# First feed-forward product: one 512-column stream of high and low token parts in place of two 256-column streams

## The chip, the cores and the metric

The kernel runs on one core of one Trainium2 chip. The metric is the device time of one execution, in microseconds (us). Three runs of the kernel before gave 906.57, 906.92 and 907.79 us; their median, 906.92 us, is the time that everything is compared with.

A core has five engines that run side by side and meet at semaphores: TensorE (PE in the profile; its weight loads stand apart as PEld), VectorE (DVE), ScalarE (ACT), GpSimd (POOL) and SyncE (SP), which here issues the loads of the weights.

## The reference, cut to what matters

Two layers run over 256 tokens of width 1024. In each, three token mixers are merged and normed; then comes the part that is changed:

```python
ffn = jnp.square(jax.nn.relu(x @ w_ff_in[i])) @ w_ff_out[i]     # 1024 -> 4096 -> 1024
ple = jax.nn.sigmoid(x @ w_ple_gate[i]) * (p[i] @ w_ple[i])
x = layer_norm(DEEPNORM_ALPHA * x + ffn + ple, ln2_g[i], ln2_b[i])
```

All inputs are float32. The kernel multiplies in TensorE's float32r type, so it writes each operand as a high part (a rounded copy) plus a low part (what the rounding left) and adds three of the four partial products: high by high, high weight by low token, low weight by high token.

## The kernel before, in words

The program is traced in Python and ordered once, when it is built: a list scheduler gives each engine a fixed queue, and the chip works through each queue in that order, waiting at semaphores. An instruction at the head of a queue that waits holds up all behind it.

**Tokens.** After the first norm, `x1T` holds the transposed tokens as two tiles of tag `t8k`, high and low, each [128, 8 blocks, 256 tokens] (`new_T`, L218; four buffers of 8 KB per partition). The same four buffers serve the tokens at the head of a layer (`xT`), the values of the attention (`vh`, `vl`), the merged branches (`mT`), and two constants at the start (`stage`, `sel_s`).

**Weights.** `wunit` (L194) loads 512 KB into a `wr` tile (3 buffers, issued on SP's queue), lets ACT write the high part `wh` (L175) and then DVE the low part `wl` (L176); `wh` and `wl` have 5 buffers each.

**PSUM.** Eight banks of 512 float32 columns: four of tag `ps`, four of tag `pg`. All four `pg` banks are the accumulators of the second half of the feed forward (`acc`, L904).

**The feed forward** (L903 to L954) goes in 8 chunks of 512 hidden channels. `ff_in(c)` makes a chunk's hidden channels with four weight units. For each of 8 blocks of input channels and each of 4 blocks `i` of 128 hidden channels it issues three products of 256 columns into half a `ps` bank (L916, L918, L919), 96 in all, into two `ps` banks. ACT then takes the relu of each bank (L924), POOL squares it (L926), and ACT and DVE split the square into parts (L928, which shows as L175 and L176). `ff_out(c)` multiplies these parts with four further weight units: 48 products of 512 columns into `acc` (L191).

The order of the chunks is `ff_in(0)`, `ff_in(1)`, `ff_out(0)`, `ff_in(2)`, `ff_out(1)`, and so on to `ff_out(7)`: only between `ff_in(0)` and `ff_in(1)` is there no `ff_out`.

Of the kernel before, what the change touches and what calls it, by code (L numbers as in the profile page):

```python
# [10 lines left out]
F32 = mybir.dt.float32  # L11
F32R = mybir.dt.float32r
# [4 lines left out]
P = 128  # L17
# [12 lines left out]
# the order of the projections, and of what goes on between their units: (job, steps to the next)  # L30
# [13 lines left out]
# columns of the combined projection  # L44
# [7 lines left out]
def hybrid_trunk(ctx, tc, x, p, w_in, b_forget, w_up_fox, w_up_sb, w_up_dsa, w_out,  # L52
# [29 lines left out]
    def t8k(dt=F32R):  # L82
        return act.tile([P, 2048], dt, tag="t8k", name=nm("t8k"), bufs=4)
# [43 lines left out]
    stage = act.tile([P, 768], F32, tag="t8k", name="stage", bufs=4)  # L127
# [6 lines left out]
    # -1 where row > column  # L134
# [3 lines left out]
    # [1 where row <= column | 1]  # L138
# [6 lines left out]
    # +BIG where column > row, over [tile 0 | tile 1: 0, diagonal]  # L145
# [4 lines left out]
    # per head h, rows h and 32 + h: ones; rows 64 + h and 96 + h: the parts of -c of the queries  # L150
    sel = cst.tile([P, H_FOX, T], F32R, name="sel")
    sel_s = act.tile([P, H_FOX, T], F32, tag="t8k", name="sel_s", bufs=4)
# [19 lines left out]
    def split(src, hi, lo, scale=None):  # L172
        """src * scale as two float32r parts, whose sum is exact."""
        if scale is None:
            a = nc.scalar.copy(hi, src)  # L175
            b = nc.vector.tensor_sub(lo, src, hi.bitcast(F32))  # L176
            if pinned[0]:
                pinned[0] -= 1
                tc.keep_in_program_order(a)
                tc.keep_in_program_order(b)  # L180
        else:
            nc.scalar.activation(hi, src, AF.Copy if isinstance(scale, float) else AF.Identity,
                                 scale=scale)
            nc.vector.scalar_tensor_tensor(lo, src, scale, hi.bitcast(F32),
                                           op0=ALU.mult, op1=ALU.subtract)

    def mm3(o, a, b, start, stop, skip=False):
        """o += a.T @ b from the parts (hi, lo) of each."""
        prods = ((a[0], b[0]), (a[0], b[1]), (a[1], b[0]))
        for i, (l, r) in enumerate(prods):  # L190
            nc.tensor.matmul(o, l, r, start=start and i == 0, stop=stop and i == 2,  # L191
                             skip_group_check=skip)

    def wunit(srcs, nk, n):  # L194
        """Weights [P, nk, n] on chip, as parts; srcs: list of (partition slice, dram AP)."""
        raw = early.pop(0) if early else wload(srcs, nk, n)
        hi = wp.tile([P, nk, n], F32R, tag="wh", name=nm("wh"), bufs=WH)
        lo = wp.tile([P, nk, n], F32R, tag="wl", name=nm("wl"), bufs=WH)
        split(raw, hi, lo)
        return hi, lo  # L200

    def transpose_to(dst, src_list):
        """src_list: blocks [P, 128] -> the columns of psum tile dst."""
        for i, s in enumerate(src_list):
            tr = nc.tensor.transpose(dst[:, i * P:(i + 1) * P], s, ident)  # L205
            if behind:
                tc.keep_in_program_order(tr)
                behind.pop()

    def to_T(src, t, hT, lT):  # L210
        """src [P, 1024] of token tile t -> hT, lT [P, 8, 256] at its columns."""
        for g in range(2):
            q = ps()
            transpose_to(q, [src[:, (4 * g + i) * P:(4 * g + i + 1) * P] for i in range(4)])
            qv = q.rearrange("p (k t) -> p k t", t=P)
            split(qv, hT[:, 4 * g:4 * g + 4, t * P:(t + 1) * P], lT[:, 4 * g:4 * g + 4, t * P:(t + 1) * P])

    def new_T():  # L218
        return (t8k().rearrange("p (k t) -> p k t", t=T), t8k().rearrange("p (k t) -> p k t", t=T))
# [4 lines left out]
    def xstat(aT, w, l, c0, n, done, nkb=KB, nk=2, by_tile=False, mid=None):  # L224
        """done(t, psum tile) with the [tokens, n] products of token tile t; a step per unit.
        By tile: all of tile 0 first, mid() after it; the high parts of the tokens come first."""
# [45 lines left out]
    def layer_norm(t, st, gt, bt, done, out_pieces=()):  # L272
        """xs[t] <- layer norm of itself, half by half (or by pieces, to out), from its statistics."""
# [28 lines left out]
    def half_T(hT, lT):  # L302
        """What turns half j of xs[t] into its transposed parts."""
        def f(t, j):
            q = ps()
            transpose_to(q, [xs[t][:, (4 * j + i) * P:(4 * j + i + 1) * P] for i in range(4)])
            qv = q.rearrange("p (k t) -> p k t", t=P)
            split(qv, hT[:, 4 * j:4 * j + 4, t * P:(t + 1) * P], lT[:, 4 * j:4 * j + 4, t * P:(t + 1) * P])
        return f

    def ple_products(l, pn):
        """p w_ple, [tokens, 1024] by half and token tile, half by half."""
# [20 lines left out]
    # x transposed  # L333
# [6 lines left out]
    for l in range(L):  # L340
        if l:
            tc.keep_in_program_order(nc.scalar.preload_act_table_set("natural_log_exp_and_others"))
        vh = t8k()[:, 0:1792].rearrange("p (t c) -> p t c", t=2)
        vl = t8k()[:, 0:1792].rearrange("p (t c) -> p t c", t=2)

        def do_rope(t, src, nh, dst, dup=1):
            """dst [P, nh * 64] <- rope of the nh heads at src (psum)."""
# [131 lines left out]
        M = {}  # L479

        def idx_scores(t):
            nk = (t + 1) * P
            sc = act.tile([P, 256], F32, tag="sc", name=nm("sc"), bufs=2)
            n_in = 512 // nk  # heads in a bank, of one row tile
# [70 lines left out]
        # outputs of pairs of heads as parts (high, low); of the heads 10 and 11 as stacks [high; low]  # L555
# [3 lines left out]
        def values(n, m, pT):  # L559
            """The outputs of the heads n .. n + m - 1 (of all 16; one block), into oT, from the  # L560
            parts of their weights [keys, m, 384]: keys of tile 0 for all queries, keys of tile 1
            for tile 1's."""
# [16 lines left out]
        def softmax_heads(n, heads, mask):  # L579
            """heads: (parts of qT [64, 256] scaled by -SCALE, parts of kT [64, 256], extra) each."""  # L580
# [24 lines left out]
            for i in range(len(heads)):  # L605
                q = ps()
                # psum: keys of tile 0 x (queries 0, queries 1), keys of tile 1 x queries 1
# [27 lines left out]
        def sb_unit(kb):  # L635
            """Columns [sq, sk] as [sq 01, sq 23, sk 01, sk 23, sq 4 | sk 4]."""
# [18 lines left out]
        def strict(a, m):  # L655
            """a [P, m, 384] <- 0 where the key isn't before the query."""
# [5 lines left out]
        def sb_heads(hs):  # L662
# [26 lines left out]
            # sums over the later keys: those of tile 0 within it and over tile 1, those of tile 1  # L689
# [47 lines left out]
        def up_blocks(j, kbs, w, n0=0):  # L737
            """Adds the blocks kbs of heads, with the weights at columns n0 .. of w."""
# [39 lines left out]
        # the branch that comes first and its first block, the last block of each branch  # L778
# [32 lines left out]
        # job: (the products that it needs, steps before the next job, job)  # L811
# [40 lines left out]
        # a zero that comes with the last head's weights: no sigmoid between the exponentials  # L852
# [11 lines left out]
        x1T = new_T()  # L864
# [39 lines left out]
        acc = [[pg() for _ in range(2)] for _ in range(2)]  # L904

        def ff_in(c):
            pz = [ps(), ps()]
            for u in range(4):
                wt = wunit(wrows(w_ff_in, l, 2 * u, 2, c * 512, 512), 2, 512)
                for kk in range(2):  # L910
                    kb = 2 * u + kk
                    for i in range(4):
                        o = pz[i // 2][:, (i % 2) * T:(i % 2 + 1) * T]
                        hi, lo = (w[:, kk, i * P:(i + 1) * P] for w in wt)
                        rh, rl = x1T[0][:, kb, :], x1T[1][:, kb, :]
                        nc.tensor.matmul(o, hi, rh, start=kb == 0 and i % 2 == 0, stop=False,  # L916
                                         skip_group_check=True)
                        nc.tensor.matmul(o, hi, rl, start=False, stop=False, skip_group_check=True)  # L918
                        nc.tensor.matmul(o, lo, rh, start=False, stop=kb == KB - 1,  # L919
                                         skip_group_check=True)  # L920
            hs = []
            for i in range(2):
                r = t2k(F32)
                nc.scalar.activation(r, pz[i], AF.Relu)  # L924
                h = t2k(F32)
                nc.gpsimd.tensor_mul(h, r, r)  # L926
# [33 lines left out]
        for t in range(2):  # L960
            # the last tile's last half in two pieces
# [23 lines left out]
def _rope_table():  # L985
    """[128, (cos tile 0, cos tile 1, sin tile 0, sin tile 1), 64], by the positions alone."""
# [26 lines left out]
```

## Time and profile before

| | us |
|---|---|
| median of three runs | 906.92 |
| lowest, highest run | 906.57, 907.79 |
| span of the profiled execution (first to last instruction) | 907.9 |
| PE busy in the span | 890.1 (98%) |
| DVE busy | 610.4 (67%) |
| ACT busy | 475.5 (52%) |
| POOL busy | 116.1 (13%) |

Of the profiled execution only its span is recorded; it lies 0.1 us above the highest of the three runs. Of a PE row the start is what counts: products overlap in the pipeline, so a row's duration (0.28 us for 256 columns) is longer than the distance from one start to the next (0.12 us), and it is the distance that adds up to time.

### The profile page before, as it was taken

The numbers are of one execution on the slowest core, as the hardware profiler recorded it, in microseconds if no ns is written. First come the engines' busy times: TensorE is split into PE (matmuls) and PEld (weight loads), VectorE is DVE, ScalarE is ACT, GpSimd is POOL, SyncE is SP. The second block draws the span as 40 slices with busy tenths as digits, with TensorE's granted clock in tenths as the row PEclk, the third lists the DMA queues.
The fourth block names the chain that finished last, engine by engine and source line by source line (L and its number), as shares of the span: only waits on it lengthen the run. The fifth ranks groups of instructions, "written<-read, shape, count | busy, mean of one in ns | idle before, by whom it ended". The sixth has DMA issues, their size and how long they took to land.

```text
span 907.9 us, 13848 instructions
## 1 busy us (share of the span) xinstructions
PE 890.1 (98%) x5190; PEld 778.7 (86%) x5190; DVE 610.4 (67%) x1035; ACT 475.5 (52%) x719; POOL 116.1 (13%) x155
## 2 busy tenths in 40 slices
PE   6999999999999999999999999999999999999996
PEld 5999988887779999999879999788777899999995
DVE  6578888678876544444676888876789564444446
ACT  4455656766445444444355555576844454444440
POOL 5002110200012011111200120101000321111120
PEclk9999999999999999999999999999999999999999
DMA  6655465452656766656636546555346576666662
GB/s 199 197 158 128 143 188 150 137 180 93 186 178 216 210 187 186 186 187 187 218 104 200 150 120 171 158 161 166 115 143 201 167 228 190 187 187 187 186 200 75
DMA packets 79699, 154.51 MB, mean 170 GB/s; under 512 B 10096, under 2 KB 25456, under 8 KB 79632
## 3 DMA queue, kind: packets, MB, share of 16 engines
q1 hardware_dynamic: 77952, 149.04, 54.7%
q0 software_dynamic: 1680, 4.60, 1.8%
q8 instruction: 41, 0.67, 0.3%
q14 instruction: 26, 0.21, 0.1%
HBM read 152.30 MB, written 1.05 MB: 169 GB/s over the span
## 4 chain that ended last, share of the span: by engine, by line
PE 44%; DVE 3%; issue 1%; DMA 1%; ACT 1%; POOLq 0%; POOL 0%; ACTq 0%; SPq 0%; DVEq 0%
PE pg L191 23%; PE ps L919 3%; PE ps L918 3%; PE ps L916 3%; PE ps L191 3%; PE pg L233 1%; PE pg L389 1%; PE pg L391 1%; PE pg L392 1%; DVE wl L176 1%; PE pg L238 1%; DMA wr<-in_w_out_dram 1%; PE ps L205 0%; DMA wr<-in_w_in_dram 0%; PE pg L749 0%
## 5 line engine op out<-in xcount | busy, mean ns | idle before, releaser
L176 DVE TENSOR_TENSOR wl<-wr,wh 128x1024 fp32r<-128x1024 f32 (+5 forms) x303 | 350.7, 1162 | 236.0 <-ACT wh L175 234.7
L175 ACT CAST wh<-wr 128x1024 fp32r<-128x1024 f32 (+5 forms) x303 | 296.2, 982 | 309.1 <-PE pg L191 107.7
L191 PE MATMUL pg<-wh,t8k 128*128 128x512 f32 (+4 forms) x768 | 224.5, 365 | 0.0
L191 PE MATMUL pg<-wh,t2k 128*128 128x512 f32 x544 | 172.8, 394 | 1.4 <-ACT wh L175 1.2
L191 PEld LDWEIGHTS pg<-wh,t8k 128*128 128x128 f32 x768 | 140.0, 188 | 19.7 <-issue 0.5
L919 PE MATMUL ps<-t8k,wl 128*128 128x256 f32 x512 | 144.9, 283 | 0.0
L918 PE MATMUL ps<-t8k,wh 128*128 128x256 f32 x512 | 144.9, 283 | 0.0
L916 PE MATMUL ps<-t8k,wh 128*128 128x256 f32 x512 | 144.8, 283 | 0.0
L191 PE MATMUL pg<-wl,t8k 128*128 128x512 f32 (+4 forms) x384 | 138.8, 362 | 0.0
L191 PEld LDWEIGHTS pg<-wh,t2k 128*128 128x128 f32 x544 | 103.0, 190 | 23.6 <-ACT wh L175 2.1
L191 PE MATMUL pg<-wl,t2k 128*128 128x512 f32 x272 | 107.3, 395 | 2.2 <-DVE wl L176 2.2
L918 PEld LDWEIGHTS ps<-t8k,wh 128*128 128x128 f32 x512 | 98.2, 192 | 0.6
L916 PEld LDWEIGHTS ps<-t8k,wh 128*128 128x128 f32 x512 | 98.2, 192 | 0.6
L919 PEld LDWEIGHTS ps<-t8k,wl 128*128 128x128 f32 x512 | 98.2, 192 | 0.0
L191 PEld LDWEIGHTS pg<-wl,t8k 128*128 128x128 f32 x384 | 72.2, 188 | 7.9
L926 POOL TENSOR_TENSOR t2k<-t2k 128x512 f32<-128x512 f32 x32 | 40.6, 1270 | 273.9 <-ACT t2k L924 258.6
L191 PEld LDWEIGHTS pg<-wl,t2k 128*128 128x128 f32 x272 | 51.6, 190 | 13.5 <-DVE wl L176 3.4
L389 PE MATMUL pg<-t8k,wh 128*128 128x256 f32 x176 | 50.6, 287 | 0.0
L392 PE MATMUL pg<-t8k,wl 128*128 128x256 f32 x176 | 49.8, 283 | 0.0
L391 PE MATMUL pg<-t8k,wh 128*128 128x256 f32 x176 | 49.7, 283 | 0.0
L233 PE MATMUL pg<-wh,t8k 128*128 128x512 f32 x96 | 37.9, 400 | 1.0 <-ACT t8k L175 1.0
L233 PE MATMUL pg<-wl,t8k 128*128 128x512 f32 x96 | 37.9, 398 | 0.6 <-DVE small L276 0.2
(180 smaller groups left out, 1077.5 us busy)
## 6 DMA issues: line engine op xcount, KB each, us to landing
wr<-in_w_ff_in_dram SPq DMA_DIRECT2D x64, 512.0 KB, 3.8
wr<-in_w_ff_out_dram SPq DMA_DIRECT2D x64, 512.0 KB, 3.6
wr<-in_w_in_dram SPq DMA_DIRECT2D x48, 512.0 KB, 3.7
wr<-in_w_in_dram SPq DMA_DIRECT2D x32, 384.0 KB, 3.5
wr<-in_w_out_dram SPq DMA_DIRECT2D x16, 512.0 KB, 3.9
wr<-in_w_ple_gate_dram SPq DMA_DIRECT2D x16, 512.0 KB, 4.5
wr<-in_w_in_dram SPq DMA_DIRECT2D x16, 256.0 KB, 2.8
wr<-in_w_in_dram SPq DMA_DIRECT2D x8, 390.0 KB, 3.5
```

The source lines that it names most:

```text
L175: a = nc.scalar.copy(hi, src)
L176: b = nc.vector.tensor_sub(lo, src, hi.bitcast(F32))
L191: nc.tensor.matmul(o, l, r, start=start and i == 0, stop=stop and i == 2, skip_group_check=skip)
L233: nc.tensor.matmul(o[t][:, :n], tok(aT, u * nk + kk, t)[0], wt[i][:, kk, :], start=u + kk + i == 0, stop=False)
L238: nc.tensor.matmul(o[t][:, :n], tok(aT, kb, t)[1], units[kb // nk][0][:, kb % nk, :], start=False, stop=kb == nkb - 1)
L389: nc.tensor.matmul(oi, hi, rh, start=kb == 0 and i % 2 == 0, stop=False, skip_group_check=True)
L391: nc.tensor.matmul(oi, hi, rl, start=False, stop=False, skip_group_check=True)
L392: nc.tensor.matmul(oi, lo, rh, start=False, stop=kb == KB - 1, skip_group_check=True)
L916: nc.tensor.matmul(o, hi, rh, start=kb == 0 and i % 2 == 0, stop=False, skip_group_check=True)
L918: nc.tensor.matmul(o, hi, rl, start=False, stop=False, skip_group_check=True)
L919: nc.tensor.matmul(o, lo, rh, start=False, stop=kb == KB - 1, skip_group_check=True)
L926: nc.gpsimd.tensor_mul(h, r, r)
```

## The change

One pool tag is widened: `t8k` (four buffers of 8 KB) becomes `t16k` (two buffers of 16 KB), so that the high and the low part of the tokens lie in one tile, 8 KB apart, and one access pattern can run over both. Every user of the tag changes with it. In `ff_in` the two products that use the high weights become one of 512 columns, high tokens then low tokens, into a whole `ps` bank, so a chunk takes all four `ps` banks in place of two. The third product is as before and adds into the first half. Afterwards ACT copies the low half of each bank to SBUF and DVE adds the high half to it; the relu and the square are one DVE instruction in place of ACT's relu and POOL's product.

```diff
-    def t8k(dt=F32R):
-        return act.tile([P, 2048], dt, tag="t8k", name=nm("t8k"), bufs=4)
+    def t16k(dt=F32R):
+        return act.tile([P, 2, 2048], dt, tag="t16k", name=nm("t16k"), bufs=2)
...
     def new_T():
-        return (t8k().rearrange("p (k t) -> p k t", t=T), t8k().rearrange("p (k t) -> p k t", t=T))
+        return both_T()[0]
+
+    def both_T():
+        a = t16k().rearrange("p i (k t) -> p i k t", t=T)
+        return (a[:, 0], a[:, 1]), a
...
-        x1T = new_T()
+        x1T, x1_both = both_T()
...
         def ff_in(c):
-            pz = [ps(), ps()]
+            pz = [ps() for _ in range(4)]
             for u in range(4):
                 wt = wunit(wrows(w_ff_in, l, 2 * u, 2, c * 512, 512), 2, 512)
                 for kk in range(2):
                     kb = 2 * u + kk
                     for i in range(4):
-                        o = pz[i // 2][:, (i % 2) * T:(i % 2 + 1) * T]
                         hi, lo = (w[:, kk, i * P:(i + 1) * P] for w in wt)
-                        rh, rl = x1T[0][:, kb, :], x1T[1][:, kb, :]
-                        nc.tensor.matmul(o, hi, rh, start=kb == 0 and i % 2 == 0, stop=False,
-                                         skip_group_check=True)
-                        nc.tensor.matmul(o, hi, rl, start=False, stop=False, skip_group_check=True)
-                        nc.tensor.matmul(o, lo, rh, start=False, stop=kb == KB - 1,
-                                         skip_group_check=True)
+                        nc.tensor.matmul(pz[i].rearrange("p (k t) -> p k t", t=T), hi, x1_both[:, :, kb, :],
+                                         start=kb == 0, stop=False, skip_group_check=True)
+                        nc.tensor.matmul(pz[i][:, 0:T], lo, x1T[0][:, kb, :], start=False,
+                                         stop=kb == KB - 1, skip_group_check=True)
             hs = []
             for i in range(2):
                 r = t2k(F32)
-                nc.scalar.activation(r, pz[i], AF.Relu)
+                for k in range(2):
+                    z, rk = pz[2 * i + k], r[:, k * T:(k + 1) * T]
+                    nc.scalar.copy(rk, z[:, T:2 * T])
+                    nc.vector.tensor_add(rk, z[:, 0:T], rk)
                 h = t2k(F32)
-                nc.gpsimd.tensor_mul(h, r, r)
+                nc.vector.scalar_tensor_tensor(h, r, 0.0, r, op0=ALU.max, op1=ALU.mult)
                 pr = (t2k(), t2k())
                 split(h, *pr)
```

The values `vh` and `vl` of the attention and the two constants at the start (`stage`, `sel_s`) move to the new tag as well. The rest of the diff takes out comments.

## Rows read from the trace of the kernel before

**Rows 1.** The page, section 1: busy time, share of the span, instructions.

```profile
PE 890.1 (98%) x5190; PEld 778.7 (86%) x5190; DVE 610.4 (67%) x1035; ACT 475.5 (52%) x719; POOL 116.1 (13%) x155
```

**Rows 2.** Both first chunks, layer 0: length, PE to POOL busy, clock, DMA, GB/s.

```profile
275.40:298.40 23.00, 23.00 (x193) 22.99 (x192) 16.21 (x14) 12.64 (x16) 6.31 (x4) 1.00 0.70 213
```

**Rows 3.** Timeline of PE: first products of the first four half-chunks (start, duration, line).

```profile
275.41 0.28 PE L916 MATMUL ps<-t8k,wh 128*128 128x256 f32 x1
...
286.92 0.28 PE L916 MATMUL ps<-t8k,wh 128*128 128x256 f32 x1
...
298.44 0.40 PE L191 MATMUL pg<-wh,t2k 128*128 128x512 f32 x1
...
309.35 0.28 PE L916 MATMUL ps<-t8k,wh 128*128 128x256 f32 x1
```

**Rows 4.** Timeline of PE: twelve products over gapped operands, and the next.

```profile
646.26 2.25 PE L191 MATMUL ps<-t3k,t8k 128*128 128x512 f32 x12
648.35 0.40 PE L191 MATMUL pg<-wh,t1k 128*128 128x512 f32 x1
```

**Rows 5.** Timeline of ACT after ff_in(0) of layer 0, brackets: idle before, releaser.

```profile
287.26 1.05 ACT L175 CAST wh<-wr 128x1024 fp32r<-128x1024 f32 x1 [1.73 <-DMA wr<-in_w_ff_in_dram]
288.21 0.59 ACT L924 ACTIVATE t2k<-ps 128x512 f32<-128x512 f32 x1
288.70 1.04 ACT L175 CAST wh<-wr 128x1024 fp32r<-128x1024 f32 x1
...
291.03 0.59 ACT L924 ACTIVATE t2k<-ps 128x512 f32<-128x512 f32 x1
```

**Rows 6.** Timeline of DVE in the same stretch.

```profile
288.34 1.23 DVE L176 TENSOR_TENSOR wl<-wr,wh 128x1024 fp32r<-128x1024 f32 x1 [1.56 <-ACT wh L175]
```

**Rows 7.** Timeline of SP: issue of the load behind the cast at 287.26.

```profile
282.36 0.37 SPq L97 DMA_DIRECT2D wr<-in_w_ff_in_dram  x1
```

**Rows 8.** The same place in layer 1: PE, ACT, DVE.

```profile
731.99 0.28 PE L916 MATMUL ps<-t8k,wh 128*128 128x256 f32 x1
...
732.39 1.05 ACT L175 CAST wh<-wr 128x1024 fp32r<-128x1024 f32 x1 [1.78 <-DMA wr<-in_w_ff_in_dram]
733.34 0.59 ACT L924 ACTIVATE t2k<-ps 128x512 f32<-128x512 f32 x1
...
733.47 1.23 DVE L176 TENSOR_TENSOR wl<-wr,wh 128x1024 fp32r<-128x1024 f32 x1 [1.60 <-ACT wh L175]
```

**Rows 9.** Lines by form: count, busy us, mean ns, idle before, releasers.

```profile
L175 ACT CAST t2k<-pg 128x256 fp32r<-128x256 f32 x6 | 2.0, 373 | 0.1
L176 DVE TENSOR_TENSOR t2k<-pg,t2k 128x256 fp32r<-128x256 f32 x6 | 2.3, 416 | 0.0
L893 DVE SCALAR_TENSOR_TENSOR x<-x,t2k 128x512 f32<-128x512 f32 x8 | 5.5, 690 | 7.1 <-POOL t2k L891 7.1
```

**Rows 10.** The last chunk: timelines of ACT and DVE, chain of waits.

```profile
877.51 0.60 ACT L924 ACTIVATE t2k<-ps 128x512 f32<-128x512 f32 x1 [1.23 <-PE ps L919]
...
883.21 0.68 DVE L176 TENSOR_TENSOR t2k<-t2k,t2k 128x512 fp32r<-128x512 f32 x1
...
878.19 16.36 PE pg L191 x72
```

**Rows 11.** Start of the span: PE at 9 and 17 us, DVE, ACT.

```profile
9.16 0.63 PE L191 MATMUL pg<-wh,t2k 128*128 128x512 f32 x1
9.59 0.63 PE L191 MATMUL pg<-wl,t2k 128*128 128x512 f32 x1
...
17.24 0.39 PE L233 MATMUL pg<-wh,t8k 128*128 128x512 f32 x1
17.47 0.39 PE L233 MATMUL pg<-wl,t8k 128*128 128x512 f32 x1
...
4.99 1.48 DVE L162 CAST cT<-stage 64x128 fp32r<-64x128 f32 x1
...
15.44 0.59 ACT L175 CAST t8k<-ps 128x512 fp32r<-128x512 f32 x1 [0.27 <-PE ps L205]
```

More of the change, by code (lines that the diff above doesn't have):

```diff
@@ L126, in hybrid_trunk @@
     nc.vector.memset(eps_t[0:64, 1:2], SCALE)
-    stage = act.tile([P, 768], F32, tag="t8k", name="stage", bufs=4)
+    stage = act.tile([P, 768], F32, tag="t16k", name="stage", bufs=2)
     def tri(ap, n, keep, fill, op, base, cm, step):
@@ L151, in hybrid_trunk @@
     sel = cst.tile([P, H_FOX, T], F32R, name="sel")
-    sel_s = act.tile([P, H_FOX, T], F32, tag="t8k", name="sel_s", bufs=4)
+    sel_s = act.tile([P, H_FOX, T], F32, tag="t16k", name="sel_s", bufs=2)
     nc.gpsimd.memset(sel_s, 0.0)
@@ L342, in hybrid_trunk @@
             tc.keep_in_program_order(nc.scalar.preload_act_table_set("natural_log_exp_and_others"))
-        vh = t8k()[:, 0:1792].rearrange("p (t c) -> p t c", t=2)
-        vl = t8k()[:, 0:1792].rearrange("p (t c) -> p t c", t=2)
+        vhl = t16k()[:, :, 0:1792].rearrange("p i (t c) -> p i t c", t=2)
+        vh, vl = vhl[:, 0], vhl[:, 1]
         def do_rope(t, src, nh, dst, dup=1):
```

## The prediction

> **What bounds the kernel now.** I read the busy shares first: PE is busy 98% of the span, DVE 67%, ACT 52% [rows 1]. A share is only an average, so the table by stretches comes next: in the two first chunks of layer 0, PE is busy 23.00 of 23.00 us at a granted clock of 1.00, with the DMA engines at 0.70 [rows 2]. PE alone sets the time there, and work on ACT, DVE or POOL costs time only where PE comes to wait for it.
>
> Then the timeline of PE, read by starts. A first-half chunk takes 286.92 - 275.41 = 11.51 us for 96 products of 256 columns, 0.1199 us each; a second-half chunk 309.35 - 298.44 = 10.91 us for 48 products of 512 columns, 0.2273 us each [rows 3]. Twice the columns cost less than twice the time: the line through both points is 0.4195 ns per column and 12.5 ns per product. Those 12.5 ns are what this change can win.
>
> **What the change removes.** Per chunk, 64 products of 256 columns become 32 of 512: 32 x (2 x 0.1199 - 0.2273) = 0.40 us, and 0.40 x 16 chunks in both layers = 6.4 us, all of it on the bound engine. The new moving operand has two runs 8 KB apart, which the second half's operands have not. The nearest row is the weighted sum of the attention's values, whose moving operand also has two gapped runs: six products of 512 columns and six of 256 take 648.35 - 646.26 = 2.09 us, 0.348 us for a pair of one each [rows 4], where the two averages above make 0.347. So the gap is free there, and by this row the gain is 16 x (11.51 - 32 x 0.348) = 6.0 us. I take 6.4 and keep 5.9 to 6.4.
>
> The Trainium skill has a smaller price for a product: TensorE: Matmul & The Clock Gate, section "Wait — 56ns, not 53.3ns?", gives a fixed cost of about 2.5 ns on top of the columns. By it the estimate would be 512 x 2.5 ns = 1.3 us in place of 6.4. The distances above disagree by a factor of five, and they decide.
>
> **What it adds.** Each chunk now fills four `ps` banks, and there are four. Between most chunks this costs nothing: a second half of 10.91 us, which writes only `pg` banks, lies between one first half and the next, and emptying the banks is shorter. In the last chunk, where the squares are needed soonest, the work from ACT's first read at 877.51 to DVE's last part at 883.21 + 0.68 = 883.89 fits into 6.4 us [rows 10]; the change turns two reads of 512 columns into four copies at 0.373 us on ACT and four additions at 0.416 us on DVE, and moves the squares from POOL to DVE at about 0.69 us each [rows 9]. That is 4 x 0.416 + 2 x 0.69 = 3.0 us more for DVE; even in series it ends by 887, and the second half that reads these squares begins 10.9 us after 878.19, at 889.1. Cover: that second half. If it were gone, 6 to 9 us per chunk would show.
>
> It is gone once per layer: `ff_in(1)` follows `ff_in(0)` directly. Before, the second one took the two free banks; now its first product needs the bank that ACT and DVE must first empty. So a wait is added on PE, and behind it on PE's queue stands all that follows.
>
> **How long that wait is.** Shortened, `ff_in(0)` ends at 275.41 + 11.11 = 286.52. On ACT's queue of before, the relu of the first bank is not next: a weight cast for `ff_in(1)` stands ahead of it, waits 1.73 us for its transfer and runs from 287.26; the relu comes at 288.21, though its bank was complete at 286.92 - 0.84 + 0.28 = 286.36 (the last product into it is seven before the next chunk's first [rows 3]) [rows 5]. That transfer was issued at 282.36 [rows 7] and does not depend on PE's pace, so it lands no sooner after the change. On DVE the subtraction of the same weights runs 288.34 to 289.57 [rows 6]. If the scheduler keeps the order, the first copy starts at 288.2 and the first addition only at 289.5; the bank is free at 289.5 + 0.42 = 289.95, and PE has waited 3.4 us. In layer 1 the end is 731.99 - 0.40 = 731.59, the subtraction ends at 733.47 + 1.23 = 734.70, the bank is free at about 735.05: 3.5 us [rows 8]. Behind the first bank the second keeps PE's pace of 0.35 us, but the first square (0.69 us, ready then and earlier in program order) probably precedes the third bank's addition. That adds 0.65 us, or nothing if PE's queue is filled with products of the free banks instead, or up to 2.0 if the cast at 288.70 (1.04 us [rows 5]) and its subtraction also come between. I take 0.65, since squares stand before later banks in the program.
>
> Sum: 2 x (3.45 + 0.65) - 6.4 = +1.8 us, between 2 x 3.4 - 6.4 = +0.4 and 2 x 5.5 - 5.9 = +5.1. The span of 907.9 lies 1.0 above the median; I apply the difference to the median: 908.7, with 907.3 to 912.0.
>
> The Trainium skill speaks against the change here: Perfetto Trace Analysis, section "Matmuls", wants independent groups to rotate through PSUM banks, so that one is emptied while the next is written. Here it holds in 14 of 16 chunks only.
>
> **Edits with one answer.** Square on DVE: POOL's 32 products go and DVE has 33% idle. The wider tag: the pairs were taken and freed together before, so it changes nothing but the start, where `xT` now reuses the buffer of `stage`; its last reader ends at 6.47 us and `xT` is first written at 15.44 [rows 11]. If the scheduler put that reader later, it could cost up to 1 us.
>
> **Rivals.**
> - *The copies overtake the cast* (the other side: faster). The queue order is fixed when the kernel is built. If all four copies stand ahead of that weight cast, the first bank is copied and added while `ff_in(0)` still writes the last: it is complete some 0.9 us before the end, and 0.373 + 0.416 us fit. What remains per layer is the third and fourth bank, 0.5 to 1.3 us. Time: -6.4 + 1.0 to -5.9 + 2.6, so 901.5 to 903.6, about 902.5. For it: a copy precedes the cast in program order, and the first bank is ready earlier than the relu's two halves were. Against it: the cast stood ahead of the relu in both layers [rows 5, 8]. It decides by whether the cast is ready, in the order made at build time, before the first bank is.
> - *Half of that*: the first copies ahead, the rest behind the cast, or one layer each way. Wait about 2.4 us per layer: 906.9 - 6.4 + 4.8 = 905.3 (904.5 to 907).
> - *The wait lowers PE's clock.* The rows of before hold no idle time of PE near 3.5 us except at the start, where products of 512 columns start 0.43 us apart at 9 us, the lower level of 1.2 GHz (though the row's granted clock says 1.00), and 0.23 us apart at 17 us [rows 11]. If 5.2 us of streaming after each wait ran at that level, it would cost 2 x 2.6 us on top of the forecast: 913.9, and with half of that 911.3. For it: between 275 and 298 us PE has no idle time at all [rows 2], so the trace can't vouch for a wait there. The Trainium skill's page TensorE: Matmul & The Clock Gate (section "What's actually happening") says that an idle TensorE falls to half rate; no run here shows it for a wait of this length.
> - *The long product does not stream.* If two runs 8 KB apart cost as much as two products, nothing is won and 2 x 4.1 us are lost: 915.1. Against it stand rows 4. With the 2.5 ns of the Trainium skill (the page named above) it would be near 913.8, which I count here.
>
> **How the numbers follow.** Forecast 46%, copies overtake 23%, half 12%, clock 14%, no gain 5%. About 0.2% (1.8 us) is what a measurement of this kernel can tell from no change: the bounds are 905.1 and 908.7. Faster: 23 + 4 (of the half) = 27%. Same: 20 (of the forecast) + 8 = 28%. Slower: 26 + 14 + 5 = 45%. The range takes the overtaking case down to 902.0 and the clock case to 912.5; outside it lie 5% below and some 11% above. The forecast's own range is 907.3 to 912.0.
>
> **What would show it.** Step one: a first-half chunk behind a second half takes 11.1 us from start to start, and pairs of products start 0.347 us apart. Step two: PE's waits list about 3.5 us twice, on its first product of `ff_in(1)`, released by DVE's addition, and nowhere else. Step three: on ACT the copies stand behind the cast that waits for its transfer. The prediction is wrong if the copies stand ahead of it (then near 902.5), if other chunks wait for banks, if products behind the wait start 0.43 us apart, or if the long product takes over 0.23 us.

## The result and the profile after

| | before | after |
|---|---|---|
| median of all runs (us) | 907.27 (906.57 to 909.31, 10 runs) | 913.26 (907.9 to 914.68, 10 runs) |
| ratio to before, 95% interval | 1 | 1.0056 (1.0043 to 1.007) |
| span of the profiled execution | 907.9 | 911.6 (its own time 913.28) |

The change makes the kernel 6.0 us slower by the two medians, and 5.1 us by the ratio, which is not the quotient of the medians. The forecast was 908.7 with a range to 912.5: the side is right, the size is not. The median lies 0.8 us above that range; but the range was set against 906.92, and counted from there (+6.0 against +5.6 by the medians, 1.0056 x 906.92 = 912.0 by the ratio) the time lies at its upper end.

The page's line of busy times answers to [rows 1]. The second line is the page's group of the new long product (count, busy us, mean ns, idle time before it and its releaser):

```profile
PE 888.5 (97%) x4678; PEld 752.4 (83%) x4678; DVE 651.4 (71%) x1131; ACT 478.8 (53%) x751; POOL 75.6 (8%) x123
...
L921 PE MATMUL ps<-t16k,wh 128*128 128x512 f32 x512 | 184.3, 403 | 6.1 <-DVE t2k L931 6.1
```

PE has 512 instructions fewer, and 6.1 us of idle time that it had not. PE's list of waits (engine and line, what it waited for: total us, times, longest) says where; its other waits are those at the kernel's other stages, and none is in the feed forward:

```profile
PE ps L921 <- DVE t2k L931: 6.1, 2, 3.4
PE ps L322 <- DMA pn<-in_p_dram: 3.8, 1, 3.8
PE pg L192 <- DVE wl L177: 1.2, 1, 1.2
PE pg L192 <- ACT wh L176: 1.2, 1, 1.2
```

Two waits, one in each layer, both on the first product of `ff_in(1)`, both ended by an addition. In PE's timeline (start, duration, line, operands; brackets: idle before, releaser) the end of `ff_in(0)` and the products behind the wait, first layer 0, then layer 1:

```profile
283.94 0.40 PE L921 MATMUL ps<-t16k,wh 128*128 128x512 f32 x1
284.17 0.28 PE L923 MATMUL ps<-t16k,wl 128*128 128x256 f32 x1
287.07 0.50 PE L921 MATMUL ps<-t16k,wh 128*128 128x512 f32 x1 [2.62 <-DVE t2k L931]
...
288.74 0.63 PE L921 MATMUL ps<-t16k,wh 128*128 128x512 f32 x1
289.17 0.41 PE L923 MATMUL ps<-t16k,wl 128*128 128x256 f32 x1
289.38 0.63 PE L921 MATMUL ps<-t16k,wh 128*128 128x512 f32 x1
...
731.65 0.28 PE L923 MATMUL ps<-t16k,wl 128*128 128x256 f32 x1
735.37 0.67 PE L921 MATMUL ps<-t16k,wh 128*128 128x512 f32 x1 [3.44 <-DVE t2k L931]
735.84 0.41 PE L923 MATMUL ps<-t16k,wl 128*128 128x256 f32 x1
736.05 0.63 PE L921 MATMUL ps<-t16k,wh 128*128 128x512 f32 x1
...
736.69 0.63 PE L921 MATMUL ps<-t16k,wh 128*128 128x512 f32 x1
```

From start to start, less the usual 0.12 us behind a short product, PE loses 287.07 - 284.17 - 0.12 = 2.78 us and 735.37 - 731.65 - 0.12 = 3.60 us. Then comes a second loss: at 288.74 and at 736.05 a pair of products takes 0.64 us instead of 0.353. The table by stretches shows the clock (length; busy us of PE, PEld, DVE, ACT, POOL with counts; granted clock; DMA share; GB/s). The four stretches are `ff_in(0)` and `ff_in(1)` of layer 0, then of layer 1:

```profile
273.00:284.30 11.30, 11.30 (x65) 9.69 (x63) 8.06 (x7) 4.97 (x6) 3.25 (x2) 1.00 0.70 219
287.00:300.00 13.00, 12.93 (x65) 11.15 (x65) 8.89 (x14) 5.67 (x9) 0.00 (x0) 0.87 0.45 143
720.40:731.80 11.40, 11.40 (x66) 9.73 (x64) 8.40 (x8) 5.56 (x7) 3.66 (x2) 1.00 0.65 199
735.30:748.30 13.00, 12.93 (x65) 11.20 (x66) 8.90 (x14) 5.67 (x9) 0.00 (x0) 0.87 0.46 143
```

Before, the clock was 1.00 and PE busy throughout here [rows 2]. Now the same 64 products take 12.93 us behind the wait and 11.29 without one, with the clock at 0.87 on average: part of the stretch ran at 1.2 GHz. That is 2 x 1.64 = 3.3 us.

The gain shows in the twelve first halves that stand alone. The first product of one, and that of the second half behind it (compare [rows 3], where 11.51 us lie between them):

```profile
310.89 0.39 PE L921 MATMUL ps<-t16k,wh 128*128 128x512 f32 x1
311.12 0.28 PE L923 MATMUL ps<-t16k,wl 128*128 128x256 f32 x1
311.23 0.40 PE L921 MATMUL ps<-t16k,wh 128*128 128x512 f32 x1
...
322.18 0.40 PE L192 MATMUL pg<-wh,t2k 128*128 128x512 f32 x1
...
333.12 0.39 PE L921 MATMUL ps<-t16k,wh 128*128 128x512 f32 x1
```

322.18 - 310.89 = 11.29 us, the same in all twelve: 0.22 us per chunk, 3.5 us for sixteen, where 0.40 and 6.4 were forecast. The second half behind it takes 333.12 - 322.18 = 10.94 us instead of 10.91; over both layers the second halves give back 0.3 us.

The sum, without those 0.3 us: -3.5 + (2.78 + 3.60) + 3.3 = +6.2 us, against +6.0 between the medians. The spans differ by 3.6 only, because this profiled execution of after was 2.4 us ahead before the feed forward: its `ff_in(0)` starts at 273.00, that of before at 275.41 [rows 3], as PE came to its upper clock earlier at the start of the span. That differs from run to run (b3 below, a changed kernel, starts its `ff_in(0)` at 275.51) and is no part of the change. In the runs where both are recorded a time is 1.6 to 1.8 us above its span, so the profiled execution of before, with a span of 907.9, took about 909.6 us, which fits its late start.

### The profile page after: what moved, and what is told of

Read it like the earlier page. It is cut to its first block, busy times and chain, and to the rows that moved or that the text cites. A ratio compares the mean times of both kernels' runs of the same rounds, so it can differ in the third digit from the quotient of the medians.

```text
span 911.6 us, 12926 instructions
## 1 busy us (share of the span) xinstructions
PE 888.5 (97%) x4678; PEld 752.4 (83%) x4678; DVE 651.4 (71%) x1131; ACT 478.8 (53%) x751; POOL 75.6 (8%) x123
## 4 chain that ended last, share of the span: by engine, by line
PE 43%; DVE 3%; DMA 2%; issue 1%; ACT 1%; POOL 1%; POOLq 0%; ACTq 0%
PE pg L192 22%; PE ps L921 6%; PE ps L192 3%; PE ps L923 3%; PE pg L239 1%; DVE wl L177 1%; PE pg L395 1%; PE pg L398 1%; PE pg L397 1%; DMA wr<-in_w_ff_in_dram 1%; PE pg L244 1%; ACT wh L176 1%; PE ps L206 1%; POOL t2k L897 0%; DMA wr<-in_w_out_dram 0%
## 5 line engine op out<-in xcount | busy, mean ns | idle before, releaser
L192 PE MATMUL pg<-wh,t16k 128*128 128x512 f32 (+4 forms) x768 | 224.4, 365 | 0.0
L921 PE MATMUL ps<-t16k,wh 128*128 128x512 f32 x512 | 184.3, 403 | 6.1 <-DVE t2k L931 6.1
L192 PEld LDWEIGHTS pg<-wh,t16k 128*128 128x128 f32 x768 | 140.0, 188 | 19.7 <-issue 0.5
L923 PE MATMUL ps<-t16k,wl 128*128 128x256 f32 x512 | 144.8, 283 | 0.0
L192 PE MATMUL pg<-wl,t16k 128*128 128x512 f32 (+4 forms) x384 | 138.8, 362 | 0.0
L921 PEld LDWEIGHTS ps<-t16k,wh 128*128 128x128 f32 x512 | 97.5, 191 | 30.7 <-DVE t2k L931 6.7
L923 PEld LDWEIGHTS ps<-t16k,wl 128*128 128x128 f32 x512 | 98.2, 192 | 0.7
L192 PEld LDWEIGHTS pg<-wl,t16k 128*128 128x128 f32 x384 | 72.2, 188 | 7.9
L395 PE MATMUL pg<-t16k,wh 128*128 128x256 f32 x176 | 50.6, 288 | 0.0
L397 PE MATMUL pg<-t16k,wh 128*128 128x256 f32 x176 | 49.7, 283 | 0.0
L395 PEld LDWEIGHTS pg<-t16k,wh 128*128 128x128 f32 x176 | 33.6, 191 | 0.3
L397 PEld LDWEIGHTS pg<-t16k,wh 128*128 128x128 f32 x176 | 33.7, 191 | 0.0
```

Of the source, the lines that this page charges most:

```text
L395: nc.tensor.matmul(oi, hi, rh, start=kb == 0 and i % 2 == 0, stop=False, skip_group_check=True)
L397: nc.tensor.matmul(oi, hi, rl, start=False, stop=False, skip_group_check=True)
L921: nc.tensor.matmul(pz[i].rearrange("p (k t) -> p k t", t=T), hi, x1_both[:, :, kb, :], start=kb == 0, stop=False, skip_group_check=True)
L923: nc.tensor.matmul(pz[i][:, 0:T], lo, x1T[0][:, kb, :], start=False, stop=kb == KB - 1, skip_group_check=True)
```

## The experiments

All times are medians beside the kernel before on the same chip (907.13, 907.45, 906.99 and 906.94 us for the groups a, b, c and d); the bracket is the 95% interval of the ratio to it, which again is not the quotient of the two medians.

| label | median | ratio to before | first half (us) |
|---|---|---|---|
| a1_change_again | 914.03 | 1.0063 (1.0046 to 1.0081) | 11.29 |
| a2_first_two_as_before | 905.21 | 0.9976 (0.9966 to 0.9986) | 11.29 |
| a3_fill_the_wait | 909.67 | 1.0029 (1.0019 to 1.0039) | 11.29 |
| a4_one_run | 913.89 | 1.0063 (1.0047 to 1.008) | 11.29 |
| b1_split_on_pool | 911.41 | 1.0041 (1.0027 to 1.0055) | 11.29 |
| b2_swap_banks | 903.65 | 0.9958 (0.9946 to 0.9971) | 11.29 |
| b3_swap_low_products_grouped | 904.42 | 0.9958 (0.9946 to 0.997) | 11.20 |
| b4_swap_low_products_one_late | 903.53 | 0.9955 (0.9942 to 0.9968) | 11.29 |
| c1_swap_grouped_one_run | 902.31 | 0.995 (0.9937 to 0.9963) | 11.20 |
| c2_swap_banks_again | 904.13 | 0.9964 (0.9951 to 0.9976) | 11.29 |
| d1_swap_groups_of_8 | 901.33 | 0.9942 (0.9927 to 0.9956) | 11.15 |
| d2_swap_groups_of_16 | 900.61 | 0.9943 (0.9924 to 0.9962) | 11.11 |

### The change again

> The changed kernel once more, timed beside the three experiments on the same chip. Expected 5 to 6.5 us above the kernel before: a gain of 0.22 us in each of 16 first-half chunks (3.5), against two waits of 2.8 and 3.6 us and twice 1.65 us in which the chunk behind the wait runs at a lower clock. If the difference to the kernel before is under 3 us, the first comparison was a matter of the chip or of the hour.

6.9 us above before. In its profiled execution the waits cost 3.17 and 3.43 us and `ff_in(1)` 13.93 and 12.79 us: -3.5 + 6.6 + 4.1 = +7.2. The two waits add up to much the same (6.4 and 6.6); what follows them at the lower clock does not (1.5 to 2.6 us per layer in the two profiles), which fits the wide spread of after's times.

### Where the loss sits

```diff
-            pz = [ps() for _ in range(4)]
+            short = c < 2
+            pz = [ps() for _ in range(2 if short else 4)]
...
+                        if short:
+                            o = pz[i // 2][:, (i % 2) * T:(i % 2 + 1) * T]
...
+                            nc.tensor.matmul(o, hi, rl, start=False, stop=False, skip_group_check=True)
...
+                if short:
+                    nc.scalar.activation(r, pz[i], AF.Relu)
```

> The first two chunks of each layer keep the three products of 256 columns in two banks and the relu on ScalarE; the other six are as changed. So no first half needs a bank that is still being emptied. Theory (waits and the clock behind them cost 9.7 us, each long-product chunk gains 0.22): no wait on an addition in PE's list, the granted clock stays 1.00 between 270 and 300 us, and the time is that of before less 12 x 0.22 = 2.7 us. Rival (the long product itself, or VectorE's larger load, makes the kernel slower): above the kernel before, by about 12/16 of the change's loss.

1.9 us below before, interval 1.3 to 3.1, which holds the 2.7 of the theory. The wait on the addition is gone from PE's list, and the second chunk, like the first, is again what it was:

```profile
284.70:296.20 11.50, 11.50 (x98) 11.50 (x97) 8.35 (x9) 7.76 (x10) 0.00 (x0) 1.00 0.70 218
```

So the long product, the copies, the additions and the squares on DVE gain in twelve chunks; all of the loss comes from the two chunks in each layer that follow each other directly.

### The clock, apart from the wait

```diff
+            if c == 1:
+                for _ in range(12):
+                    nc.tensor.matmul(acc[0][0].rearrange("p (k t) -> p k t", t=T), last_w[0],
+                                     x1_both[:, :, 0, :], start=True, stop=True, skip_group_check=True)
```

In `ff_in(1)` the loop also takes the first two banks through three weight blocks before the other two, since the queue of the changed kernel, too, works on the first two banks for a while before it touches the third.

> The changed kernel, with twelve additional products of 512 columns (2.8 us at 0.235 each) between ff_in(0) and ff_in(1), written to an accumulator that the first real product of ff_out(0) overwrites. They use operands that are there already, so PE streams during the wait in place of idling, while ACT and VectorE empty the banks in the same queue order. Theory (idling lowers the clock, and that costs 1.65 us per layer by itself): the products behind the wait start at the pace of 0.353 us per pair, the granted clock stays at 1.00, and the time is 3.3 us below that of the changed kernel. Rival (the lower clock there has another cause, such as the change of operands or of banks): the clock falls as before and the time is not below that of the changed kernel.

4.4 us below the changed kernel. The products that fill the wait, and what comes behind them:

```profile
284.20 2.94 PE L919 MATMUL pg<-t16k,wl 128*128 128x512 f32 x12
287.25 0.50 PE L934 MATMUL ps<-t16k,wh 128*128 128x512 f32 x1
287.58 0.28 PE L936 MATMUL ps<-t16k,wl 128*128 128x256 f32 x1
287.70 0.40 PE L934 MATMUL ps<-t16k,wh 128*128 128x512 f32 x1
287.94 0.28 PE L936 MATMUL ps<-t16k,wl 128*128 128x256 f32 x1
288.06 0.40 PE L934 MATMUL ps<-t16k,wh 128*128 128x512 f32 x1
```

The table by stretches, for `ff_in(1)`:

```profile
287.20:298.70 11.50, 11.45 (x65) 9.95 (x66) 8.90 (x13) 5.66 (x9) 0.00 (x0) 1.00 0.43 143
```

PE is held up about as long as in after (287.25 - 284.20 = 3.05 us, and 2.78 in layer 1), but it streams meanwhile; behind it pairs start about 0.355 us apart and the clock is 1.00. Idling, not the new operands or banks, lowers the clock here. From `ff_in(0)` to the end of `ff_in(1)` the two layers take 25.75 and 25.45 us, 6.0 more than four chunks of 11.29; -3.5 + 6.0 = +2.5, and the median is +2.5 above before. The 4.4 us to a1 are about what the lower clock cost there (4.1 by the traces) and its longer waits (6.6 against 6.0). The Trainium skill, TensorE: Matmul & The Clock Gate, section "What's actually happening", has an idle TensorE fall to half rate; this pair of runs agrees.

### The queue order in front of the copies

```diff
+                if c == 1 and u == 3:
+                    raw = wload(wrows(w_ff_in, l, 2 * u, 2, c * 512, 512), 2, 512)
...
+                    nc.gpsimd.tensor_copy(wt[0], raw)
+                    nc.gpsimd.tensor_sub(wt[1], raw, wt[0].bitcast(F32))
```

> The changed kernel, with the split of the last weight block of ff_in(1) (cast and subtraction) on GpSimd in place of ScalarE and VectorE, in both layers. The four copies and additions that empty the banks then have no weight cast ahead of them that waits for its transfer. Theory (the wait is long because the copies stand behind that cast): the wait on the addition falls from 2.6 and 3.4 us to under 1 us per layer, the clock does not fall, and the time is about 905 us (907.1 - 16 x 0.22 + 2 x 0.8 = 905.2). Rival (the wait is the work of emptying itself, wherever the cast stands): the wait stays above 2 us, and the time stays near that of the changed kernel, 913 to 914. A third outcome: GpSimd needs so long for the split that the products of that block wait for it, near the end of ff_in(1).

Neither theory nor rival: 911.41. The first wait falls as the theory says, and a second one takes its place. Timelines of layer 0 (L928 is the long product, L938 the addition, L921 here GpSimd's subtraction):

```profile
284.20 0.75 DVE L938 TENSOR_TENSOR t2k<-ps,t2k 128x256 f32<-128x256 f32 x2
...
284.67 0.50 PE L928 MATMUL ps<-t16k,wh 128*128 128x512 f32 x1 [0.23 <-DVE t2k L938]
...
286.59 1.05 ACT L176 CAST wh<-wr 128x1024 fp32r<-128x1024 f32 x1 [2.44 <-DMA wr<-in_w_ff_out_dram]
...
286.66 2.39 POOL L921 TENSOR_TENSOR wl<-wr,wh 128x1024 fp32r<-128x1024 f32 x1
...
287.67 2.46 DVE L177 TENSOR_TENSOR wl<-wr,wh 128x1024 fp32r<-128x1024 f32 x1 [1.99 <-ACT wh L176]
...
290.65 0.74 DVE L938 TENSOR_TENSOR t2k<-ps,t2k 128x256 f32<-128x256 f32 x2
...
291.21 0.47 PE L928 MATMUL ps<-t16k,wh 128*128 128x512 f32 x1 [2.86 <-DVE t2k L938]
```

The two subtractions in layer 1, and then the stretches behind the second wait in layer 0 and in layer 1:

```profile
731.99 2.73 POOL L921 TENSOR_TENSOR wl<-wr,wh 128x1024 fp32r<-128x1024 f32 x1
733.14 2.67 DVE L177 TENSOR_TENSOR wl<-wr,wh 128x1024 fp32r<-128x1024 f32 x1 [0.68 <-ACT wh L176]
...
291.20:299.00 7.80, 7.79 (x45) 6.86 (x46) 5.56 (x8) 4.49 (x6) 0.00 (x0) 1.00 0.59 190
737.00:746.00 9.00, 9.00 (x44) 7.82 (x45) 5.34 (x7) 4.47 (x6) 0.00 (x0) 0.84 0.52 162
```

With no cast ahead of them the copies and additions of the first two banks are done at once, and PE waits 0.23 us. But the next cast in ACT's queue, for the second half's weights, also waits for its transfer; its subtraction stands on DVE ahead of the additions for the third and fourth bank, and takes 2.46 us instead of 1.23. PE runs out of products for the first two banks and waits 2.86 us (2.47 in layer 1). The two chunks take 26.04 and 27.08 us, 8.0 more than four of 11.29: -3.5 + 8.0 = +4.5, measured +4.0. So the split ahead of the copies and additions (the cast on ACT with its subtraction on DVE) set the length of the first wait: shown. Getting ahead of it did not win the wait back here.

The subtraction is slow only in the shadow of GpSimd's: it ends 290.13, 1.08 us after GpSimd's at 286.66 + 2.39 = 289.05; in layer 1 likewise, 735.81 after 734.72. The Trainium skill, SBUF — State Buffer, section "SBUF: two separate sides", says that a VectorE instruction with two SBUF inputs and a GpSimd one that reads SBUF lock each other out for a whole instruction. Both places agree; there the split could not be moved free of charge. So part of the second wait is this run's own doing. An estimate takes off what the subtraction took too long, 2.46 - 1.23 = 1.23 us in layer 0 and 1.44 in layer 1; 1.6 and 1.0 us of the second waits are left, which the next cast in the queue would have caused by itself.

### Another bank instead of a shorter wait

```diff
+    role = ["ps", "pg"]
...
-        return psp.tile([P, 512], F32, tag="ps", name=nm("ps"), bufs=4)
+        return psp.tile([P, 512], F32, tag=role[0], name=nm("ps"), bufs=4)
...
+            if c == 1:
+                role.reverse()
             hs = ff_in(c)
+            if c == 1:
+                acc += [[pg() for _ in range(2)] for _ in range(2)]
```

`pg()` takes its tag from `role[1]` in the same way, and the accumulators are taken only behind `ff_in(1)`, so that `ff_in(1)` writes the four banks that `ff_in(0)` has not touched.

> All 16 first halves as changed, but before ff_in(1) of each layer the two sets of four banks change roles: ff_in(1) takes the four that are still free, and the accumulators of the second half take those that ff_in(0) has used, once they are emptied. Theory (only the bank makes ff_in(1) wait): no wait on an addition, the granted clock stays 1.00, ff_in(1) takes 11.3 us, and the time is 907.1 - 16 x 0.22 = 903.6 us. Rival (with the two first halves back to back, ff_in(1) waits for its weights instead, at ScalarE and VectorE, which have no pause there): the time stays above 905.2.

903.65, as the theory says; once more with c2: 904.13.

> The changed kernel with swapped banks once more, to compare with the grouped one on the same chip. Expected: 903 to 904.5 us, 11.29 us per first half.

The stretch of `ff_in(1)` in layer 0 of b2, with no wait in front of it and none in it:

```profile
284.50:295.80 11.30, 11.30 (x66) 9.80 (x65) 8.94 (x13) 7.71 (x13) 0.00 (x0) 1.00 0.58 196
```

The weights are there in time: ACT 7.71 and DVE 8.94 of 11.30 us busy. Layer 1 is the same, 11.30 us at a clock of 1.00. So the wait was for the bank alone.

### The missing half of the gain

The forecast took 0.347 us for a pair of one long and one short product; it is 0.353. Where do the 6 ns come from? First, one run of 512 columns in place of two:

```diff
-        a = t16k().rearrange("p i (k t) -> p i k t", t=T)
-        return (a[:, 0], a[:, 1]), a
+        a = t16k().rearrange("p i n -> p (i n)").rearrange("p (k i t) -> p k i t", i=2, t=T)
+        return (a[:, :, 0], a[:, :, 1]), a
```

> The changed kernel, with the transposed tokens laid out so that the high and the low part of one block stand side by side: the 512 columns of the long product are one run instead of two runs 8 KB apart. The waits stay. Theory (the second run costs about 6 ns per product): a first-half chunk behind a second half takes 11.1 us instead of 11.29, and the time is 16 x 0.18 = 2.9 us below that of the changed kernel. Rival (the pair costs 0.353 us for another reason, such as the alternation of lengths): the chunk stays at 11.29 and the time does not move.

11.29 us still, and no difference to a1. The gap of 8 KB costs nothing here. Next, in b4 each short product comes one product later, so that no two products into one bank follow each other, and in b3 the four long products of a block come first and the four short ones behind them:

> The kernel with the swapped banks; each product of 256 columns comes one product later than before, so lengths still alternate but two products into the same bank never follow each other. If the bank is what costs the 6 ns per pair, a first half takes 11.1 us; if the turn of lengths does, 11.29, while the grouped order gains; if both stay at 11.29, it is neither.

> The kernel with the swapped banks; in each block of tokens the four products of 512 columns come first and the four of 256 columns after them, in place of one of each in turn. So seven of eight products follow one of their own length, and none follows a product into the same bank. The pair has cost 0.353 us where a row of equal products makes 0.347. Theory A (the surplus of 6 ns comes from the turn of lengths or from two products into one bank behind each other): a first half takes 11.15 us instead of 11.29, and the time is 16 x 0.14 = 2.2 us below the swapped kernel. Theory B (it belongs to the 512-column product with this operand): 11.29 as before and no difference in time.

b4 stays at 11.29: it is not the bank. b3 falls to 11.20: the turn of lengths costs something. Its median is not below b2's, because its five times fall into two groups, 902.1 to 902.3 and 904.4 to 904.9; in the profiled one `ff_in(0)` starts at 275.51 instead of 273.23, the difference at the start of the span met above. b3 with one run of columns:

> Swapped banks, products grouped by length, and the 512 columns of the long product as one run. With the lengths in turn, one run cost as much as two (11.29 us), and the grouped order with two runs took 11.20: its long products start 0.2326 us apart behind each other, where the one-run products of the second half start 0.2277 apart. Theory (two runs cost 5 ns a product, which the turn of lengths hides): the long products start 0.228 apart, a first half takes 11.07 us, and the time is 16 x 0.13 = 2.1 us below the swapped kernel with two runs and 16 x 0.22 = 3.5 us below the swapped kernel in the old order, that is near 900.8 in comparison with 903.6. Rival (the operand's layout never matters): 11.20 as in the grouped order.

11.20 again, so the layout does not matter in this order either; the theory is refuted, and the median's 1.8 us below c2 are the grouping's 16 x 0.09 = 1.4 within the error. Then longer groups, sixteen of a kind as shown here, and eight:

```diff
+            for u0 in range(0, 4, 2):
...
+                for kb in range(2 * u0, 2 * (u0 + 2)):
+                    for i in range(4):
+                        nc.tensor.matmul(pz[i].rearrange("p (k t) -> p k t", t=T),
...
+                for kb in range(2 * u0, 2 * (u0 + 2)):
+                    for i in range(4):
+                        nc.tensor.matmul(pz[i][:, 0:T], wts[kb // 2 - u0][1][:, kb % 2, i * P:(i + 1) * P],
```

> Swapped banks; in each weight block of 256 rows the eight products of 512 columns come first and then the eight of 256 columns (groups of four before). In the second half of the kernels before and after, the first four to ten long products start 0.231 to 0.240 us apart and the rest 0.227. Theory (the long product reaches 0.227 only after some products of its own length): with groups of eight a first half takes 11.20 or a little less, about 11.17. Rival (each turn of lengths costs a fixed 12 ns, of which groups of four save three in four): half as many turns again save 0.01 to 0.02 us, 11.18. So this run alone tells little, and the next one tells them apart.

> The same with groups of sixteen. Theory (0.227 after some products): the last six or more long products of each group start 0.227 apart, a first half takes about 11.10, and the time is 16 x 0.19 = 3.0 us below the swapped kernel in the old order, if ScalarE and VectorE have the weights ready (two blocks are now needed ahead of the first low product, and the wait for them can take all of it). Rival (a fixed cost per turn, and a long product at 0.233 with this operand or with changing banks): 0.233 throughout and 11.18.

11.15 and 11.11. PE's timeline of one first half of d2, between the last product of a second half and the first of the next (equal products are joined; the distance of two starts gives the pace):

```profile
328.22 0.39 PE L194 MATMUL pg<-wh,t2k 128*128 128x512 f32 x1
328.44 3.79 PE L921 MATMUL ps<-t16k,wh 128*128 128x512 f32 x16
332.07 2.08 PE L926 MATMUL ps<-t16k,wl 128*128 128x256 f32 x16
333.98 3.82 PE L921 MATMUL ps<-t16k,wh 128*128 128x512 f32 x16
337.64 2.08 PE L926 MATMUL ps<-t16k,wl 128*128 128x256 f32 x16
339.55 0.40 PE L194 MATMUL pg<-wh,t2k 128*128 128x512 f32 x1
```

The same in b3, where a first half begins:

```profile
308.86 1.07 PE L922 MATMUL ps<-t16k,wh 128*128 128x512 f32 x4
309.77 0.64 PE L925 MATMUL ps<-t16k,wl 128*128 128x256 f32 x4
310.24 1.09 PE L922 MATMUL ps<-t16k,wh 128*128 128x512 f32 x4
```

The first sixteen long products of d2, behind long ones of the second half, run at (332.07 - 328.44) / 16 = 0.2269 us; the second sixteen, behind short ones, at 0.2288. By the single start times the first five distances of these are 0.233, 0.236, 0.228, 0.233 and 0.231 us and all others 0.226 or 0.227; in d1 every later group begins with nearly the same five. They stood in the trace of before already: every second half there, which follows short products (the first at 298.44 [rows 3]), opens with 0.233, 0.236, 0.228, 0.233 and 0.231 us and goes on at 0.226 or 0.227. Behind first halves with the lengths in turn (after) a second half opens with ten slow ones, 0.224 to 0.241 us, and that is its 0.03 us more. In b3, too, the group behind the second half runs at (309.77 - 308.86) / 4 = 0.2275, and over all its groups a long product behind another takes 0.2326. With lengths in turn (after) no long product gets past this: 0.236, and 0.117 for the short one. So the theory holds against the fixed cost per turn with an operand that stays slow. Why five products behind short ones are slower stays open; operand layout and bank are excluded.

At 900.61 us, 6.3 below before, d2 has the lowest median here; its interval overlaps that of d1.

## Why the prediction came out as it did

- *The twelve first halves that stand alone, 11.11 us each, gain 6.4 in all.* Mis-sized: 11.29 and 3.5. The step that failed is the price of a pair, 0.347 us, put together from rows of products of one length and taken as confirmed by [rows 4]. That row counts twelve products in one number; by their single starts they come three of a length at a time, and only the second three long ones, at 0.233, 0.236 and 0.228 us, follow short ones. A turn's price could be read there and at the head of each second half of before. The 12.5 ns per product from [rows 3] were right: d2, with 32 products fewer per chunk and few turns, takes exactly the 11.11 of the forecast. The 2.5 ns that the Trainium skill gives (TensorE: Matmul & The Clock Gate, "Wait — 56ns, not 53.3ns?") would, as an estimate, have made it 11.51 - 32 x 0.0025 = 11.43. The trace disagrees, and it decides.
- *PE waits once per layer, on the bank, behind a cast and its subtraction.* Right in place and order; b1 and b2 show both. That the cast waits for its transfer holds in layer 1, where ACT's and DVE's timelines stand as forecast from [rows 8]. In layer 0, the first row here, the profile puts its start down to a long product of PE instead; the last one of `ff_in(0)` ends at 283.94 + 0.40 = 284.34:

```profile
284.38 1.04 ACT L176 CAST wh<-wr 128x1024 fp32r<-128x1024 f32 x1 [1.53 <-PE ps L921]
...
732.67 1.04 ACT L176 CAST wh<-wr 128x1024 fp32r<-128x1024 f32 x1 [1.81 <-DMA wr<-in_w_ff_in_dram]
733.63 0.64 ACT L930 COPY t2k<-ps 128x256 f32<-128x256 f32 x2
...
733.75 1.23 DVE L177 TENSOR_TENSOR wl<-wr,wh 128x1024 fp32r<-128x1024 f32 x1 [1.64 <-ACT wh L176]
734.89 0.75 DVE L931 TENSOR_TENSOR t2k<-ps,t2k 128x256 f32<-128x256 f32 x2
```

- *3.4 and 3.5 us for the first bank.* Measured 2.78 and 3.60. `ff_in(0)` ended 0.18 us later than forecast; counted from its start, the cast came 0.47 us sooner in layer 0 (284.38 - 273.00 against 287.26 - 275.41) and 0.29 later in layer 1.
- *0.65 us for the later banks.* Nothing, though in layer 0 the additions for them start 3.1 us behind the first ones (289.73 against 286.60): PE's queue holds more products for the first two banks. In b1 it runs 19 of them and then waits for the third bank; after has the same sequence of lengths there. The prediction named this outcome and did not take it.
- *The clock stays up.* This is the step that turned +1.8 into +6. It had a rival at 14%, priced at 2.6 us per layer and near 911.3 to 913.9; measured 1.5 to 2.6, with a time of 913.3. The 5.2 us of streaming behind that price stand on no row. The rows of before could not say whether the clock falls; that this rival, which rests on the same wait as the forecast, did not count for more was the choice that failed. The range's upper end, 912.5, near which the time lies, was set by this rival. Without the clock the measured terms give -3.5 + 6.4 = +2.9 (a3: +2.5), near the +1.8 of the forecast because two errors, 2.9 too much gain and 1.8 too much wait, partly cancel; that is luck.
- *The copies overtake the cast, 902.5.* It did not happen. b1 shows that the third bank is then held by the next cast, as the rival allowed for with 0.5 to 1.3 us per layer; the 1.6 and 1.0 us estimated there are not far from it, but no run has the copies ahead of the cast with both on their old engines, so its price stays open.
- *Steady chunks, squares on DVE, the tag:* nothing, as forecast; a2 and b2 show it. DVE is busy 651 us instead of 610, an addition takes 0.42 us and a square 0.69 as [rows 9] had it, and no product of the feed forward outside the two places waits for them.

## What to carry to other kernels

A product that needs twice the banks is paid for where two such stages follow each other; look for the place where the cover is missing, and give the second stage banks that are already free before shortening what empties them. A wait of PE costs more than its length, since the products behind it can run at the lower clock; price both together. To win the fixed cost of a product by joining two, keep products of one length behind each other: in turn with short ones nearly half the gain was lost here.

## What the runs showed of the hardware that was not expected

- Long products behind short ones: the first five start 0.228 to 0.236 us apart, later ones 0.227 (d1, d2, and the second halves of before).
- The clock after a wait: by the brackets of the timelines, 2.62 and 3.44 us of idle PE in after were each followed by pairs at 0.64 us, that is 1.2 GHz, and so were 2.12 us in layer 1 of a4. In b1 2.86 us left the clock at 1.00 in layer 0, and 2.47 us were followed by 0.84 in layer 1 (stretches of 7.8 and 9.0 us behind them). Near this length the wait alone does not decide it; what does stays open.
- VectorE's subtraction of 1.23 us takes 2.46 and 2.67 us when one of GpSimd's is under way (b1).
